# 342 dense tokens instead of 352, three lanes of 42 instead of four of 32, gate chunks of 18 instead of 16

## The chip, the core and the metric

The kernel runs on one core of a Trainium2 chip. The metric is the device time of one execution in microseconds (us). Of the kernel before there are three runs, with a median of 2845.26 us (2840.71 to 2845.80).

## What is computed

One decoder layer on 512 tokens of 2048 float32 channels: a convolution group and a sliding-window attention group, an output projection with a residual, and then the PEER channel mixer, which the change is about. PEER chooses 128 of 16384 single-neuron experts for each token (8 heads, 16 each) with a gate for each, and adds up their outputs:

```
def chunk_fn(args):                                    # xc: tokens, ec: chosen experts, gc: gates
    xc, ec, gc = args
    u_sel = jnp.take(peer_u, ec, axis=0)
    h = jnp.einsum("cd,chkd->chk", xc, u_sel)
    a = jax.nn.gelu(h, approximate=False) * gc
    v_sel = jnp.take(peer_v, ec, axis=0)
    return jnp.einsum("chk,chkd->cd", a, v_sel)
```

## The kernel before

The input projection, convolution, attention, output projection and the choice of experts run for all 512 tokens in the first third of the time. PEER then treats the tokens in two ways, at the same time.

**Dense tokens** (TD = 352). For these the kernel multiplies with all 16384 experts and lets a gate of zero remove those that were not chosen. TensorE (PE) works through 128 *expert tiles* (`expert_tile`, L957): a tile is 128 experts, two weight units of 1024 columns, 16 chunks of the channels, and three products a chunk (high by high, high by low, low by high parts), so 48 matmuls with TD columns each. The first 64 tiles (AHEAD = 8 groups of 8) only store their activations to DRAM (`H`). The other 64 tiles multiply them by the gates (`gated`, L998) and fold them straight into the output (`fold_group`, L1003: 8 steps a group, 48 matmuls a step, two banks that VectorE adds to `acc`, L1024). At the end the 8 stored groups come back and are folded. That is 12288 matmuls with TD columns, 6 lines (L965, L967, L968, L1014, L1016, L1017) with 2048 each.

**Weights.** `stream` (L129) loads pairs of units by SyncE's queue; for each unit ScalarE (ACT) writes the rounded high part `w_hi` (L153) and VectorE (DVE) the rest `w_lo` (L154), into rings of three buffers. A unit's `w_hi` can therefore only be written when TensorE is through with the unit three before it. 116 units are used ahead of expert tile 0, so tile e uses units 116+2e and 117+2e.

**Gates.** For the dense tokens `dense_gates` (L921) builds the dense gate rows, four tokens a call: VectorE makes one-hot rows `oh` (L930, two buffers), ScalarE scales four of them to `og` (L933), TensorE makes four products into one PSUM bank `gps` (L937), and ScalarE copies the bank into the chunk `gt` (L938). A chunk of GT = 16 tokens is written to DRAM (`G`, L940). 88 calls are handed out over the first 64 tiles by `pump`, which spends an allowance of 6.2 a tile on entries with a cost (3.4 a call); `drain` (L981) hands out the rest after tile 63. The pools of this stage are closed behind it; the pool `mg`, in which the first `hv` (the eviction of tile 64) lies, takes their place. Each group loads its gates `Gb` from `G` (L992). There are four `mm` banks, so tile 68 can start when tile 64 has been evicted.

**Gathered tokens.** The last 128 tokens have a token on each partition and take 128 gathers for `peer_u` and 128 for `peer_v`; NB = 32 further tokens are spread over LANES = 4 lanes of 32 partitions, with SB = 32 gathers for each table. A gather step (`gather_step`, L872) is one indirect load of 128 rows of 8 KB by GpSimd (POOL, L862) into one of three buffers (two `grow` and the unused one of `xrow`/`yrow`), and one pass of VectorE over 128x2048 (L884 for the products with `peer_u`, L894 for the sums with `peer_v`). There are STEPS = 320 steps. `step` (L951) spreads them over ticks 3 to 247 of 256; a tick is one expert tile or one fold step. What is left is handed out by L1061 after the last fold. Then the lanes are added up by four matmuls with `fold_s` (`yo`, L1072) and stored.

The order of the instructions on each engine is set at build time by a list scheduler that simulates the program; each engine then works through its own list strictly in order.

## Time and profile before

| | |
|---|---|
| median of three runs | 2845.26 us |
| the profiled execution | 2844.32 us |
| its span | 2842.5 us |
| TensorE busy | 2809.8 us (99%) |
| VectorE busy | 2367.0 us (83%) |
| ScalarE busy | 1209.9 us (43%) |
| GpSimd busy | 449.1 us (16%) |
| mean granted TensorE clock | 0.996 |
| moved by DMA | 761.06 MB |

Times in the rows are microseconds from the start of the span. A row of the timeline gives start, duration, engine, line and operation, output and inputs, how many instructions were merged, and in brackets the idle time of that engine before it with what ended it. In the tables by stretch each engine has its busy time and, as (x), the instructions that began there; then come the granted clock of TensorE (1.00 is full speed), the mean busy share of the 16 DMA engines, and what they moved.

### The profile page before, as it was taken

What the parts mean: (1) busy time and instruction counts of PE and PEld (TensorE: products, weight loads), DVE (VectorE), ACT (ScalarE), POOL (GpSimd) and SP (SyncE); (2) the same over time, 40 slices, a digit from 0 to 9 for tenths busy, and PEclk for the clock granted to TensorE, in tenths of its full rate; (3) what the DMA queues carried; (4) which work ended last, traced back from release to release, by engine and by line L of the source; (5) the groups of instructions that cost most, each with busy time, mean ns of one, the idle gap of its engine ahead of it and who ended that gap; (6) DMA issues with size and microseconds to landing.
All of it is one profiled execution on the core that took longest, in us unless ns stands there. A gap on an engine that the chain in (4) does not pass through costs nothing.

```text
span 2842.5 us, 42927 instructions
## 1 busy us (share of the span) xinstructions
PE 2809.8 (99%) x16995; PEld 2691.1 (95%) x16995; DVE 2367.0 (83%) x3586; ACT 1209.9 (43%) x1879; POOL 449.1 (16%) x337
## 2 busy tenths in 40 slices
PE   8999999999999999999999999999999999999999
PEld 8998877788899999999999999999999999999999
DVE  7888996569999988887777888788788888888886
ACT  5666434343343378786323333233333333333332
POOL 0000000000022212111222222222121221221231
PEclk9999999999999999999999999999999999999999
DMA  5222322433278889999899898888888898888886
GB/s 172 79 67 75 112 96 76 165 123 134 80 283 329 337 316 334 325 323 337 341 352 343 313 360 325 330 335 327 330 323 337 322 371 322 349 331 337 324 332 239
DMA packets 166762, 761.06 MB, mean 268 GB/s; under 512 B 14432, under 2 KB 66784, under 8 KB 90208
## 3 DMA queue, kind: packets, MB, share of 16 engines
q1 hardware_dynamic: 66432, 377.20, 35.5%
q0 software_dynamic: 46080, 335.56, 31.4%
q10 hardware_dynamic: 54048, 45.56, 4.9%
q8 instruction: 133, 2.18, 0.3%
q14 instruction: 69, 0.57, 0.1%
...
## 4 chain that ended last, share of the span: by engine, by line
PE 95%; DVE 3%; issue 1%; ACT 1%; DMA 0%; DVEq 0%; SPq 0%
PE mm L1014 11%; PE mm L1016 11%; PE mm L1017 11%; PE mm L967 11%; PE mm L968 11%; PE mm L965 11%; PE gps L937 3%; PE mm L600 2%; PE mm L601 2%; PE mm L817 2%; PE mm L819 2%; PE mm L818 2%; PE mm L512 2%; PE mm L511 2%; PE mm L510 2%; PE mm L599 2%
## 5 line engine op out<-in xcount | busy, mean ns | idle before, releaser
L153 ACT ACTIVATE w_hi<-w_raw 128x1024 fp32r<-128x1024 f32 x628 | 665.0, 1060 | 1289.9 <-PE mm L1016 630.5
L154 DVE TENSOR_TENSOR w_lo<-w_raw,w_hi 128x1024 fp32r<-128x1024 f32 x628 | 772.6, 1232 | 291.0 <-ACT w_hi L153 283.2
L967 PE MATMUL mm<-nl,w_hi 128*128 128x352 f32 x2048 | 664.5, 324 | 0.0
L965 PE MATMUL mm<-nh,w_hi 128*128 128x352 f32 x2048 | 662.9, 324 | 1.0 <-ACT w_hi L153 1.0
L968 PE MATMUL mm<-nh,w_lo 128*128 128x352 f32 x2048 | 660.2, 324 | 2.2 <-DVE w_lo L154 2.2
L1014 PE MATMUL mm<-ah,w_hi 128*128 128x352 f32 x2048 | 658.1, 323 | 2.7 <-DVE acc L1024 2.7
L1016 PE MATMUL mm<-al,w_hi 128*128 128x352 f32 x2048 | 660.2, 323 | 0.0
L1017 PE MATMUL mm<-ah,w_lo 128*128 128x352 f32 x2048 | 652.0, 322 | 1.4 <-DVE w_lo L154 1.4
L968 PEld LDWEIGHTS mm<-nh,w_lo 128*128 128x128 f32 x2048 | 384.8, 188 | 3.1 <-DVE w_lo L154 2.8
L1014 PEld LDWEIGHTS mm<-ah,w_hi 128*128 128x128 f32 x2048 | 384.1, 188 | 3.8 <-DVE acc L1024 2.7
L965 PEld LDWEIGHTS mm<-nh,w_hi 128*128 128x128 f32 x2048 | 385.3, 188 | 1.5 <-ACT w_hi L153 1.3
L967 PEld LDWEIGHTS mm<-nl,w_hi 128*128 128x128 f32 x2048 | 385.2, 188 | 0.1
L1017 PEld LDWEIGHTS mm<-ah,w_lo 128*128 128x128 f32 x2048 | 383.3, 188 | 2.0 <-DVE w_lo L154 2.0
L1016 PEld LDWEIGHTS mm<-al,w_hi 128*128 128x128 f32 x2048 | 384.7, 188 | 0.0
L862 POOL DMA_INDIRECT grow<-un,idx x87 | 119.5, 1373 | 855.1 <-DVE grow L884 403.5
L894 DVE SCALAR_TENSOR_TENSOR xrow<-grow,h,xrow 128x2048 f32<-128x2048 f32 x86 | 201.8, 2347 | 0.0
L884 DVE SCALAR_TENSOR_TENSOR grow<-grow,xrow 128x2048 f32<-128x2048 f32 x87 | 199.5, 2294 | 2.1 <-DMA grow<-un,idx 2.1
L862 POOL DMA_INDIRECT grow<-vn,idx x86 | 109.1, 1269 | 455.2 <-DVE xrow L894 439.3
L307 DVE SCALAR_TENSOR_TENSOR mix_c<-h,par,mix_c 128x512 f32<-128x512 f32 x240 | 173.7, 749 | 1.6
L1024 DVE TENSOR_TENSOR acc<-acc,mm 128x352 f32<-128x352 f32 x240 | 116.4, 518 | 65.8 <-PE mm L1017 65.7
L933 ACT ACTIVATE og<-oh,kt 128x128 f32<-128x128 f32 x352 | 110.4, 392 | 18.2 <-DVE oh L930 10.5
L930 DVE TENSOR_TENSOR oh<-iof,kt 128x1024 f32<-128x1024 f32 x88 | 105.9, 1221 | 11.7 <-PE gps L937 11.0
...
## 6 DMA issues: line engine op xcount, KB each, us to landing
w_raw<-ut SPq DMA_DIRECT2D x128, 1024.0 KB
w_raw<-vt SPq DMA_DIRECT2D x128, 1024.0 KB
...
```

The lines of the kernel that those rows point to most:

```text
L153: nc.scalar.activation(hi, raw, AF.Copy)
L154: nc.vector.tensor_tensor(lo, raw, hi.bitcast(FT), op=OP.subtract)
L307: nc.vector.scalar_tensor_tensor(mix_c[:, c], h[:, k:k + T], w, mix_c[:, c], op0=OP.mult, op1=OP.add)
L862: i = nc.gpsimd.indirect_dma_start(out=g, out_offset=None, in_=src, in_offset=bass.IndirectOffsetOnAxis(ap=at, axis=0))
L884: nc.vector.scalar_tensor_tensor(g, g, 1.0, rows["x"][:p], op0=OP.mult, op1=OP.mult, accum_out=h3[:p, k:k + 1])
L894: nc.vector.scalar_tensor_tensor(y, g, h3[:p, k:k + 1], y, op0=OP.mult, op1=OP.add)
L965: m = nc.tensor.matmul(bank, hi[:, s], nh[:, k, :TD], start=k == 0, stop=False)
L967: nc.tensor.matmul(bank, hi[:, s], nl[:, k, :TD], start=False, stop=False)
L968: nc.tensor.matmul(bank, lo[:, s], nh[:, k, :TD], start=False, stop=k == KC - 1)
L1014: m = nc.tensor.matmul(banks[j], hi[:, ws], ah[:, ee], start=ee == 0, stop=False)
L1016: nc.tensor.matmul(banks[j], hi[:, ws], al[:, ee], start=False, stop=False)
L1017: nc.tensor.matmul(banks[j], lo[:, ws], ah[:, ee], start=False, stop=ee == 7)
```

## The change

342 tokens are dense (TD), the other 42 (NB) go into three lanes of 42 partitions with 43 gathers each for either table (SB = 43; the 129th place is empty), so STEPS becomes 342. Every indirect load fetches 128 rows; the two partitions without a lane hold index 0 and a gate of zero. The gate chunk holds 18 tokens in 6 calls of three tokens (GQ), so there are 114 calls with a cost of 2.55. `h3` lies in another pool. Some slices start at partition 64, and buffers that lanes leave partly unwritten are cleared.

```diff
@@ -18,13 +18,13 @@
 T, D = 512, 2048
 KC = D // 128
 NT = T // 128
-TD = 352
+TD = 342
 TA = T - 128
 NB = TA - TD
-LANES = 128 // NB
-PB = LANES * NB
-SB = 128 // LANES
-GT = 16
+LANES = 3
+SB = 43
+GT = 18
+GQ = 3
 AHEAD = 8
 START = 2
 END = 247.0
@@ -666,7 +666,7 @@
         nc.scalar.activation(xrow[:, c4 * 512:c4 * 512 + 512], ps, AF.Copy)
         for src, to in ((pb, XB), (py, YB)):
             xb = xtp.tile([128, 512], FT, name="xb", bufs=1)
-            nc.scalar.activation(xb[128 - NB:], src[128 - NB:], AF.Copy)
+            nc.scalar.activation(xb[64:], src[64:], AF.Copy)
             nc.scalar.dma_start(to[:, c4 * 512:c4 * 512 + 512], xb[128 - NB:])
 
     X1 = [dram.tile([128, TD], FT, name=f"X{c}") for c in range(KC)]
@@ -791,15 +791,18 @@
         later(0.2, head_idx, h, low=True)
 
     def lane_lists():
-        ps_ = slice(128 - NB, 128)
+        ps_ = slice(64, 128)
+        nc.gpsimd.memset(idxb, 0)
+        nc.gpsimd.memset(GB3, 0.0)
         ib = kp.tile([128, 128], I32, name="ib")
         e1 = E1[ps_, 2].rearrange("p h k -> p (h k)")
         e2 = E2[ps_, 2].rearrange("p h k -> p (h k)")
-        ga = GA[ps_, 2].rearrange("p h k -> p (h k)")
+        ga = GA[128 - NB:, 2].rearrange("p h k -> p (h k)")
         nc.vector.scalar_tensor_tensor(ib[ps_], e1, 128.0, e2, op0=OP.mult, op1=OP.add)
         for l in range(LANES):
-            nc.scalar.dma_start(idxb[l * NB:l * NB + NB], ib[ps_, l * SB:l * SB + SB])
-            nc.scalar.dma_start(GB3[l * NB:l * NB + NB], ga[:, l * SB:l * SB + SB])
+            w = min(SB, 128 - l * SB)
+            nc.scalar.dma_start(idxb[l * NB:l * NB + NB, :w], ib[128 - NB:, l * SB:l * SB + w])
+            nc.scalar.dma_start(GB3[l * NB:l * NB + NB, :w], ga[:, l * SB:l * SB + w])
 
     for h in range(PH):
         kr = wqp.tile([128, 2, 128], FT, name="kr", bufs=2)
@@ -833,7 +836,7 @@
     G = dram.tile([16, 128, NCH, 8, GT], FT, name="G")
 
     pu = ctx.enter_context(tc.tile_pool(name="pu", bufs=1))
-    h3 = gat.tile([128, 128 + SB], FT, name="h3")
+    h3 = pu.tile([128, 128 + SB], FT, name="h3")
     rows = {"x": xrow, "y": None}
     STEPS = 2 * (128 + SB)
 
@@ -845,6 +848,7 @@
         if n == 128 + SB:
             nc.scalar.dma_start(t, YA)
         elif n == 128:
+            nc.gpsimd.memset(t, 0.0)
             for l in range(LANES):
                 nc.scalar.dma_start(t[l * NB:l * NB + NB], XB)
         else:
@@ -857,8 +861,7 @@
             g = pu.tile([128, D], FT, name="grow", bufs=2)
         else:
             g = gat.tile([128, D], FT, name=home[1], bufs=1)
-        at = idx[:, k:k + 1] if k < 128 else idxb[:PB, k - 128:k - 127]
-        g = g[:128 if k < 128 else PB]
+        at = idx[:, k:k + 1] if k < 128 else idxb[:, k - 128:k - 127]
         i = nc.gpsimd.indirect_dma_start(out=g, out_offset=None, in_=src,
                                          in_offset=bass.IndirectOffsetOnAxis(ap=at, axis=0))
         if after is not None:
@@ -878,20 +881,19 @@
                 nc.scalar.dma_start(out_r[NB:], rows["y"])
             rows["x" if n == 128 else "y"] = spare.pop(n)
             home.reverse()
-        p = 128 if k < 128 else PB
         if n < 128 + SB:
             g = gather(un, k, after)
-            nc.vector.scalar_tensor_tensor(g, g, 1.0, rows["x"][:p], op0=OP.mult, op1=OP.mult,
-                                           accum_out=h3[:p, k:k + 1])
-            if k % 16 == 15:
-                s = slice(k - 15, k + 1)
-                w = GA3[:, s] if k < 128 else GB3[:PB, k - 143:k - 127]
-                nc.scalar.activation(h3[:p, s], h3[:p, s], AF.Gelu)
-                nc.vector.tensor_tensor(h3[:p, s], h3[:p, s], w, op=OP.mult)
+            nc.vector.scalar_tensor_tensor(g, g, 1.0, rows["x"], op0=OP.mult, op1=OP.mult,
+                                           accum_out=h3[:, k:k + 1])
+            if k % 16 == 15 or k == 127 + SB:
+                s = slice(k - k % 16, k + 1)
+                w = GA3[:, s] if k < 128 else GB3[:, s.start - 128:s.stop - 128]
+                nc.scalar.activation(h3[:, s], h3[:, s], AF.Gelu)
+                nc.vector.tensor_tensor(h3[:, s], h3[:, s], w, op=OP.mult)
         else:
-            y = rows["y"][:p]
+            y = rows["y"]
             g = gather(vn, k, after)
-            nc.vector.scalar_tensor_tensor(y, g, h3[:p, k:k + 1], y, op0=OP.mult, op1=OP.add)
+            nc.vector.scalar_tensor_tensor(y, g, h3[:, k:k + 1], y, op0=OP.mult, op1=OP.add)
 
     done = [0]
 
@@ -921,30 +923,30 @@
 
     def dense_gates(q):
         pg, kt = gpl
-        c, part = divmod(q, GT // 4)
+        c, part = divmod(q, GT // GQ)
         if part == 0:
             gt[c] = pg.tile([128, 128, GT], FT, name="gt", bufs=2)
-        oh = pg.tile([128, 2, 4, 128], FT, name="oh", bufs=2)
-        og = pg.tile([128, 4, 128], FT, name="og", bufs=2)
-        ts = slice(4 * q, 4 * q + 4)
-        nc.vector.tensor_tensor(oh, iof[:, None, None, :].to_broadcast([128, 2, 4, 128]),
-                                kt[:, 0:2, ts, None].to_broadcast([128, 2, 4, 128]), op=OP.is_equal)
-        for i in range(4):
-            nc.scalar.activation(og[:, i], oh[:, 0, i], AF.Copy, scale=kt[:, 2, 4 * q + i:4 * q + i + 1])
+        oh = pg.tile([128, 2, GQ, 128], FT, name="oh", bufs=2)
+        og = pg.tile([128, GQ, 128], FT, name="og", bufs=2)
+        ts = slice(GQ * q, GQ * q + GQ)
+        nc.vector.tensor_tensor(oh, iof[:, None, None, :].to_broadcast([128, 2, GQ, 128]),
+                                kt[:, 0:2, ts, None].to_broadcast([128, 2, GQ, 128]), op=OP.is_equal)
+        for i in range(GQ):
+            nc.scalar.activation(og[:, i], oh[:, 0, i], AF.Copy, scale=kt[:, 2, GQ * q + i:GQ * q + i + 1])
         with tc.high_priority(offset=150):
-            ps = aux_bank([128, 4, 128], "gps")
-            for i in range(4):
+            ps = aux_bank([128, GQ, 128], "gps")
+            for i in range(GQ):
                 nc.tensor.matmul(ps[:, i], oh[:, 1, i], og[:, i], start=True, stop=True, skip_group_check=True)
-            nc.scalar.activation(gt[c][:, :, 4 * part:4 * part + 4].rearrange("p e t -> p t e"), ps, AF.Copy)
-        if part == GT // 4 - 1:
+            nc.scalar.activation(gt[c][:, :, GQ * part:GQ * part + GQ].rearrange("p e t -> p t e"), ps, AF.Copy)
+        if part == GT // GQ - 1:
             nc.scalar.dma_start(G[:, :, c].rearrange("g p e t -> p g (e t)"),
                                 gt.pop(c).rearrange("p (g e) t -> p g (e t)", e=8))
 
     later(0.0, open_gates, low=True)
     for t in range(3):
         later(0.4, transposes, t, low=True)
-    for q in range(TD // 4):
-        later(3.4, dense_gates, q, low=True)
+    for q in range(TD // GQ):
+        later(2.55, dense_gates, q, low=True)
 
     tick = [0]
 
@@ -1059,17 +1061,15 @@
             prepare(g + 1)
         fold_group(As.pop(g), 1.2, last=g == AHEAD - 1)
     gather_until(STEPS, None)
-    fold_s = mg.tile([128, LANES, NB], FT, name="fold_s")
-    nc.vector.tensor_copy(fold_s[:, 0], ident[:, 0:NB])
+    fold_s = mg.tile([128, NB], FT, name="fold_s")
+    nc.vector.tensor_copy(fold_s, ident[:, 0:NB])
     for l in range(1, LANES):
-        nc.vector.tensor_tensor(fold_s[:, 0], fold_s[:, 0], ident[:, l * NB:l * NB + NB], op=OP.add)
-    for l in range(1, LANES):
-        nc.vector.tensor_copy(fold_s[:, l], fold_s[:, 0])
+        nc.vector.tensor_tensor(fold_s, fold_s, ident[:, l * NB:l * NB + NB], op=OP.add)
     yo = pu.tile([128, D], FT, name="grow", bufs=2)
     for c4 in range(4):
         ps = aux_bank([128, 512], "yo")
         cs = slice(c4 * 512, c4 * 512 + 512)
-        nc.tensor.matmul(ps, fold_s.rearrange("p l n -> p (l n)"), rows["y"][:, cs], start=True, stop=True)
+        nc.tensor.matmul(ps[:NB], fold_s, rows["y"][:, cs], start=True, stop=True)
         nc.scalar.activation(yo[:NB, cs], ps[:NB], AF.Copy)
     nc.sync.dma_start(out_r[:NB], yo[:NB])
```

The new numbers also move instructions in the lists. In the lists below the lines of the changed kernel are L154 (`w_lo`), L153 (`w_hi`), L886 and L896 (the gather passes), L932 (`oh`), L935 (`og`), L939 (`gps`), L940 (`gt`), L942 (the write of `G`), L967/L969/L970 (an expert tile), L971 (eviction), L1002 (`gated`) and L1026 (`acc`).

TensorE, the last gate products. Before, in tile 61, between the products of the tile:

```order
L968 MATMUL mm<-nh,w_lo 128x352
L937 MATMUL gps<-og,oh 128x128
L965 MATMUL mm<-nh,w_hi 128x352
L937 MATMUL gps<-og,oh 128x128 x3
L967 MATMUL mm<-nl,w_hi 128x352
L968 MATMUL mm<-nh,w_lo 128x352
L965 MATMUL mm<-nh,w_hi 128x352
```

Now, from the end of tile 67 on; the row after the 48 is the first product of tile 68:

```order
L970 MATMUL mm<-nh,w_lo 128x342
L939 MATMUL gps<-og,oh 128x128 x3
L967 MATMUL mm<-nh,w_hi 128x342
L969 MATMUL mm<-nl,w_hi 128x342
L970 MATMUL mm<-nh,w_lo 128x342
L967 MATMUL mm<-nh,w_hi 128x342
L969 MATMUL mm<-nl,w_hi 128x342
L970 MATMUL mm<-nh,w_lo 128x342
L939 MATMUL gps<-og,oh 128x128 x48
L967 MATMUL mm<-nh,w_hi 128x342
```

The first gate products stand in tile 29 before and in tile 33 now, the last in tile 61 before and between tiles 67 and 68 now.

ScalarE at the same place. The last `w_hi` ahead of this piece is that of the first half of tile 69 (the 255th unit), and from it to the last write of `G` there are 45 `og` and 16 `gt`; this is the end of the piece, up to the next `w_hi`:

```order
L942 DMA G<-gt 128x16x144
L935 ACTIVATE og<-oh,kt 128x128
L940 ACTIVATE gt<-gps 128x3x128 x2
L935 ACTIVATE og<-oh,kt 128x128 x6
L940 ACTIVATE gt<-gps 128x3x128 x2
L935 ACTIVATE og<-oh,kt 128x128 x6
L940 ACTIVATE gt<-gps 128x3x128 x2
L942 DMA G<-gt 128x16x144
L971 ACTIVATE hv<-mm 128x342 x2
L188 ACTIVATE ah<-hv 128x342 x2
L971 ACTIVATE hv<-mm 128x342
L153 ACTIVATE w_hi<-w_raw 128x1024
```

The two evictions `hv` (tiles 64 and 65) wait for the last two writes of `G`, whose buffers lie where `hv` lies now. Before, the last write of `G` stands ahead of the eviction of tile 61.

VectorE, the end of the list. Before, one gather pass stands between the last `w_lo` and the last four `acc`, and none after:

```order
L894 SCALAR_TENSOR_TENSOR yrow<-grow,h_7303,yrow 128x2048
L1024 TENSOR_TENSOR acc<-acc,mm 128x352 x2
L154 TENSOR_TENSOR w_lo<-w_raw,w_hi 128x1024 x2
L894 SCALAR_TENSOR_TENSOR yrow<-grow,h_7303,yrow 128x2048
L1024 TENSOR_TENSOR acc<-acc,mm 128x352 x4
```

Now, from the last `w_lo` on; after the last two `acc`, which need the last product of the last fold step, 15 gather passes are left (the last four rows are the first six of them, and the other nine go on in the same pattern):

```order
L154 TENSOR_TENSOR w_lo<-w_raw,w_hi 128x1024 x2
L896 SCALAR_TENSOR_TENSOR yrow<-grow,h_7303,yrow 128x2048
L1026 TENSOR_TENSOR acc<-acc,mm 128x342 x2
L896 SCALAR_TENSOR_TENSOR yrow<-grow,h_7303,yrow 128x2048
L896 SCALAR_TENSOR_TENSOR yrow<-xrow,h_7303,yrow 128x2048
L1026 TENSOR_TENSOR acc<-acc,mm 128x342 x2
L896 SCALAR_TENSOR_TENSOR yrow<-grow,h_7303,yrow 128x2048 x2
L896 SCALAR_TENSOR_TENSOR yrow<-xrow,h_7303,yrow 128x2048
L896 SCALAR_TENSOR_TENSOR yrow<-grow,h_7303,yrow 128x2048 x2
L896 SCALAR_TENSOR_TENSOR yrow<-xrow,h_7303,yrow 128x2048
```

## Rows read from the trace of the kernel before

**Rows 1.** The page's part 1, busy time, share of the span, instructions.

```profile
PE 2809.8 (99%) x16995; PEld 2691.1 (95%) x16995; DVE 2367.0 (83%) x3586; ACT 1209.9 (43%) x1879; POOL 449.1 (16%) x337
```

**Rows 2.** Tables by stretch: later sweep, groups 8 to 15, stored groups, end.

```profile
905.00:1335.00 430.00, 428.55 (x2888) 427.90 (x2887) 364.00 (x389) 303.45 (x592) 91.22 (x59) 1.00 0.92 329
1335.00:2280.00 945.00, 942.28 (x5887) 941.17 (x5887) 756.22 (x739) 315.36 (x382) 197.50 (x160) 1.00 0.88 334
2280.00:2805.00 525.00, 523.57 (x3262) 522.99 (x3262) 454.25 (x480) 168.81 (x201) 123.72 (x79) 1.00 0.89 341
2805.00:2842.50 37.50, 33.28 (x195) 31.02 (x193) 19.81 (x18) 7.70 (x10) 0.94 (x1) 1.00 0.36 128
```

**Rows 3.** Groups by line: busy us, mean ns of one, then idle before.

```profile
L967 PE MATMUL mm<-nl,w_hi 128*128 128x352 f32 x2048 | 664.5, 324 | 0.0
L1017 PE MATMUL mm<-ah,w_lo 128*128 128x352 f32 x2048 | 652.0, 322 | 1.4 <-DVE w_lo L154 1.4
```

**Rows 4.** Timeline of PE: 22 matmuls in a row of 352 columns, first and last.

```profile
859.68 0.32 PE L965 MATMUL mm<-nh,w_hi 128*128 128x352 f32 x1
...
863.04 0.32 PE L965 MATMUL mm<-nh,w_hi 128*128 128x352 f32 x1
```

**Rows 5.** Timeline of PE: 17 matmuls in a row of 512 columns, first and last.

```profile
60.17 0.39 PE L510 MATMUL mm<-xh,w_hi 128*128 128x512 f32 x1
...
63.91 0.39 PE L511 MATMUL mm<-xl,w_hi 128*128 128x512 f32 x1
```

**Rows 6.** Chain that ended last: eight gate products, two instructions each.

```profile
1008.53 1.78 PE gps L937 x16
```

**Rows 7.** Timeline of ACT in the sweep: gate evictions, one-hot scalings, one `w_hi`.

```profile
1009.46 2.00 ACT L938 ACTIVATE gt<-gps 128x512 f32<-128x512 f32 x2 [1.25 <-PE gps L937]
...
1014.06 2.44 ACT L933 ACTIVATE og<-oh,kt 128x128 f32<-128x128 f32 x8
1016.59 1.06 ACT L153 ACTIVATE w_hi<-w_raw 128x1024 fp32r<-128x1024 f32 x1
```

**Rows 8.** Timeline of PE: its last gate products.

```profile
1332.24 0.83 PE L937 MATMUL gps<-og,oh 128*128 128x128 f32 x6
```

**Rows 9.** Timelines of ACT's and SP's queues: last `H` write, first `Gb`.

```profile
1354.91 0.34 ACTq L979 DMA_DIRECT2D H<-gl  x1
...
1361.10 0.33 SPq L992 DMA_DIRECT2D Gb<-G  x1
```

**Rows 10.** Tables by stretch, TensorE partly idle for five us, and after.

```profile
565.00:570.00 5.00, 3.72 (x22) 3.26 (x22) 1.66 (x4) 2.85 (x7) 0.00 (x0) 0.69 0.01 3
570.00:575.00 5.00, 5.00 (x18) 4.16 (x17) 3.93 (x6) 1.78 (x3) 0.00 (x0) 0.63 0.50 210
```

**Rows 11.** Timeline of DVE: two gather passes in a row; the last four `acc`.

```profile
2325.47 4.74 DVE L894 SCALAR_TENSOR_TENSOR xrow<-grow,h,xrow 128x2048 f32<-128x2048 f32 x2
...
2827.78 0.95 DVE L1024 TENSOR_TENSOR acc<-acc,mm 128x352 f32<-128x352 f32 x2
2834.41 1.00 DVE L1024 TENSOR_TENSOR acc<-acc,mm 128x352 f32<-128x352 f32 x2 [5.68 <-PE mm L1017]
```

**Rows 12.** Timeline of PE: the lane sums at the end.

```profile
2834.69 3.60 PE L1072 MATMUL yo<-yrow,fold_s 128*128 128x512 f32 x8
```

**Rows 13.** Timeline of POOL: the last gather.

```profile
2808.95 0.94 POOL L862 DMA_INDIRECT grow<-vn,idxb  x1 [6.73 <-DVE yrow L894]
```

**Rows 14.** Tables by half us: where its transfer ends.

```profile
2815.00:2815.50 0.50, 0.50 (x5) 0.50 (x4) 0.00 (x0) 0.00 (x0) 0.00 (x0) 1.00 0.44 158
2815.50:2816.00 0.50, 0.50 (x6) 0.50 (x5) 0.00 (x0) 0.38 (x1) 0.00 (x0) 1.00 0.01 3
```

**Rows 15.** Timelines of POOL and DVE: a gather that VectorE waited for.

```profile
1607.56 0.94 POOL L862 DMA_INDIRECT grow<-un,idx  x1 [10.62 <-DVE grow L884]
...
1618.68 2.29 DVE L884 SCALAR_TENSOR_TENSOR grow<-grow,xrow 128x2048 f32<-128x2048 f32 x1 [2.13 <-DMA grow<-un,idx]
```

**Rows 16.** The page's part 3, the queue of the gathers: packets, MB, share.

```profile
q0 software_dynamic: 46080, 335.56, 31.4%
```

## The prediction

> **What bounds the kernel now.** I first read the page's busy times, then the tables by stretch, then the groups and timelines of the places that the change touches. TensorE is busy 99% of the span [rows 1], at a granted clock of 1.00, the upper of its two levels (2.4 GHz), and through the whole PEER part it hardly stops: in the three stretches from 905 to 2805 us its idle time is 1900 - 1894.4 = 5.6 us [rows 2]. VectorE is at 83% there (1574 of 1900) and the DMA engines at 88 to 92% [rows 2], so both are covered by TensorE now, but not by much. The reader is to see two things: what is taken from the dense matmuls comes off the time one for one, and whatever makes TensorE stop, or work go on behind its last product, is added one for one.
>
> **Columns taken away.** The 12288 dense matmuls are six lines of 2048 [rows 3]; two of the six stand there. A row's 324 ns is the duration of a pipelined matmul; what counts is the distance between starts. 22 starts in a row take 863.04 - 859.68 = 3.36 us, 0.160 us each for 352 columns [rows 4]; 17 starts with 512 columns take 3.74 us, 0.234 us each [rows 5]. The two are in the ratio of their columns (0.455 and 0.457 ns a column), so I see no fixed part, and 10 columns fewer save 4.55 ns: 12288 x 4.55 ns = **-55.9 us**. The Trainium skill ("TensorE: Matmul & The Clock Gate", section "Back-to-back issue gap") gives N/2.4 + 2.5 ns for a warm matmul alone, 149 ns at 352 columns where the trace has 160. By it the saving would be 4.17 ns a matmul, 51.2 us instead of 55.9. The gates of ten tokens go too: a token's product is two instructions of 1.78/16 = 0.111 us [rows 6], 10 x 0.22 = **-2.2 us**.
>
> **The gate work between tiles 67 and 68.** Before, the last gate products ran at 1332 us, among the products of tile 61 [rows 8], three tiles ahead of the end of the stage. In the new list 48 of them (16 calls) stand together ahead of the first product of tile 68. ScalarE reaches this batch by the `w_hi` of the 255th unit, whose ring buffer is that of the second half of tile 67; so the batch starts when TensorE is through with tile 67. From there ScalarE has one `w_hi` of 1.06 us, 45 scalings at 2.44/8 = 0.305 (13.7 us) and 16 evictions [rows 7]. An eviction of 512 columns took 1.00 us; one of 384 lies between 0.75 (by columns) and 1.00; I take 0.8 as nearer to the columns, 12.8 us. That is 27.6 us. A call goes VectorE, ScalarE, TensorE, ScalarE through two buffers; the sweep shows up to 1.25 us of waiting in two calls [rows 7], so 0 to 10 us over the batch, and I take 4. Then the last write of `G` must land before `hv` takes its place. The nearest row is the last `H` write, 6.2 us from its issue until `Gb`, which takes its buffer, is issued [rows 9]; I bound it by 4 and 8 and take 6, since the write is larger (1.2 against 0.7 MB) but meets idle queues. With 0.6 us for the eviction, tile 68 starts 38.2 us after tile 67 ended. 48 x 0.222 = 10.7 us of that is gate products, which were paid before as well; 27.5 us is new idle time. Afterwards TensorE may meet a lower clock: after a stretch with 3.72 of 5 us busy the table shows 0.69 and 0.63 [rows 10], so part of the time at the lower level of 1.2 GHz; I put 3.5 us for it. VectorE's next `w_lo` stands behind `fold_s` and the first `gated` passes, which wait for `G` and for `Gb`; tile 68 and half of tile 69 (11.2 us) are already converted, which covers some 6 us of load and 6 us of passes closely, so 0 to 4 us more, taken as nothing. Sum **+31 us**, between 21 (no waits, short write, no clock loss) and 48 (all the upper ends).
>
> **The gathers behind the last product.** There are 342 gather steps instead of 320, and the list lets them fall behind: 15 passes stand behind the last `acc`, where before there was none. So they begin when TensorE has finished for good. `acc` ended 0.7 us after TensorE's last dense product (2834.41 + 1.00 against 2834.69) [rows 11, 12]. Two passes in a row take 4.74, so 2.37 us each [rows 11]. A buffer goes round in a pass, 0.3 us to GpSimd, and the load. For the load without the weights beside it I take the last gather: issued at 2808.95, transfer at an end by 2815.5, that is 6.5 us [rows 13, 14]. The round is 9.2 us for three gathers. The first three are loaded ahead; the fourth pass starts at 9.2, the seventh at 18.4, the tenth at 27.6, the thirteenth at 36.8, and the fifteenth ends at 43.9 us. The DMA engines allow that: a gather is 0.314 x 2842.5 / 320 = 2.79 us of all sixteen [rows 16]. Lower end: VectorE's own pace, 15 x 2.37 = 35.6 us. Upper end: the 11.1 us that a load took among the weights [rows 15], a round of 13.8 and 62 us in all. The lane sums took 3.60 us at the full clock [rows 12] and come now after 44 us of an idle TensorE, so I double them as at the lower level [rows 10], +3.6. Sum **+48 us**, between 36 and 66. The Trainium skill ("DMA: Bandwidth & Descriptors", section "Anatomy of one DMA — SWDGE (gpsimd) path") gives about 2.0 us plus the bytes at 436 GB/s for such a load, 4.4 us for its 1 MB, where the trace has 6.5. By that VectorE would set the pace and the sum would be about 8 us lower.
>
> **The rest.** 327 steps instead of 320 now lie beside a dense part that is 3% shorter, so the DMA share rises by about 0.05 and VectorE's from 0.83 to 0.86; TensorE idled 5.6 us under the present load [rows 2], and I put **+3 us**, from -5 (the present idle gone) to +20. The 26 more gate calls (each with three tokens instead of four), the clearing on GpSimd (16% busy [rows 1]), the narrower `acc` and `gated` passes and the smaller tables lie under TensorE and count nothing; if TensorE were not the bound, they would be a few us of either sign.
>
> **Sum.** -55.9 - 2.2 + 31 + 48 + 3 = +24 us, on a span of 2842.5, 2866.5; the execution's own time lies 1.8 us above its span, so 2868 us. That execution is 0.9 us below the median of the runs shown. About 0.2%, 5.7 us, is what a measurement of this kernel can tell from no change.
>
> **Rivals.**
> *The boundary costs almost nothing* (8%), the way to a faster kernel. If ScalarE and VectorE ran the batch beside tiles 65 to 67, only the write of `G` and the eviction would be left, 7 us, and with VectorE's pace in the tail (40 us with the lane sums) the sum is -58 + 7 + 40 = -11: 2833 us. It decides where boundary and tail together fall below 52 us. For it: ScalarE is busy only 303 of 430 us in the sweep [rows 2]. Against it: each engine keeps its order, and the `w_hi` ahead of the batch needs tile 67 to be finished.
> *The columns give nothing* (6%). If TensorE works in steps of 16 or 32 columns, 342 cost what 352 cost (both measured widths are multiples of 32 [rows 4, 5]), and the change doesn't do what it says: 2868 + 56 = 2924 us. The strict proportion speaks against it without excluding it; the rows of `ah`, now at multiples of 1368 bytes, could cost something of the same kind.
> *The loads become the bound* (9%). The steps come every 245 x 7.46 / 342 = 5.35 us. With 11.1 us of load the round of 13.8 allows 4.6; at 13.6 us it is 16.3, 5.43 a step, 0.08 too slow: VectorE waits, `w_lo` is late, and 327 x 0.08 = 26 us are added: 2894 us. For it: VectorE has already waited once with two buffers [rows 15]. Against it: TensorE hardly idles at a share of 0.92 [rows 2].
>
> **How the numbers follow.** The forecast has 77%. Its ends don't come together; 10 and 12 us down and 17, 18 and 17 us up, taken as independent, give about 2850 to 2898. With the third rival in, and the first two out, the range is 2846 to 2902. Faster: the first rival, 0.08. Within 0.2%: the lower ends of boundary and tail together, 0.08. Slower: 0.84.
>
> **What would show it.** Dense starts 0.1555 us apart (the columns); a gap on TensorE of some 27 us net ahead of tile 68, with ScalarE busy through it and the next `w_lo` after the first `gated`; 15 passes after the last `acc` over 36 to 62 us, with TensorE idle and the lane sums behind it at a lower clock. The prediction is wrong if tile 68 follows tile 67 within 15 us, if the tail is under 30 us, or if starts stay 0.160 us apart.

## The result, and the profile after

The changed kernel takes 2895.85 us (median of 4 runs, 2894.89 to 2898.28) against 2845.53 us for the kernel before on the same chip: ratio 1.0181, 95% interval 1.0169 to 1.0194. I had forecast 2868 us, so slower was right and +24 us was half of the +50 us measured. The profiled execution took 2896.28 us, its span is 2894.5 us, 52.0 us longer than before's, where the forecast had +24.

The page's part 1 of the changed kernel answers to [rows 1]:

```profile
PE 2777.1 (96%) x16975; PEld 2652.3 (92%) x16975; DVE 2409.3 (83%) x3642; ACT 1213.1 (42%) x1896; POOL 498.7 (17%) x362
```

The tables by stretch answer to [rows 2] (window; length; busy us and count on PE, PEld, DVE, ACT, POOL; granted clock; DMA share; GB/s):

```profile
905.00:1335.00 430.00, 425.40 (x2865) 425.04 (x2865) 367.35 (x426) 277.90 (x525) 98.98 (x65) 1.00 0.97 339
1335.00:2280.00 945.00, 920.47 (x5838) 916.81 (x5837) 757.03 (x750) 344.04 (x464) 202.46 (x158) 0.99 0.88 330
2280.00:2805.00 525.00, 517.63 (x3286) 515.96 (x3286) 451.27 (x481) 169.45 (x203) 121.30 (x79) 1.00 0.91 341
2805.00:2894.50 89.50, 31.57 (x172) 26.63 (x170) 56.19 (x33) 6.84 (x9) 26.98 (x18) 0.68 0.76 245
```

TensorE was idle 5.6 us in the first three stretches before; now it is idle 4.6 + 24.5 + 7.4 = 36.5 us there, and 57.9 us in the last. The waits of PE name where (released by; us in total, times, longest):

```profile
PE yo L1072 <- DVE yrow L896: 52.7, 1, 52.7
PE gps L939 <- ACT og L935: 15.9, 11, 4.6
PE mm L967 <- ACT hv L971: 9.5, 1, 9.5
PE mm L1019 <- DVE w_lo L154: 7.4, 6, 4.8
```

**Columns.** The timeline of PE, 28 products of 342 columns in a row, first and last, answers to [rows 4]:

```profile
1507.72 0.32 PE L969 MATMUL mm<-nl,w_hi 128*128 128x342 f32 x1
...
1511.95 0.32 PE L969 MATMUL mm<-nl,w_hi 128*128 128x342 f32 x1
```

That is 4.23 us over 27 distances, 156.7 ns each, where 352 columns took 160.0; other quiet stretches of the sweep and of the fold have 156.6 to 156.7 as well. A product saves 3.3 ns and not 4.55: 12288 x 3.33 = 40.9 us instead of 55.9.

**Boundary.** Tables by stretch, then the timelines of ACT (with its queue) and of PE where tile 68 begins:

```profile
1335.00:1375.00 40.00, 33.18 (x206) 31.85 (x204) 31.48 (x33) 29.93 (x63) 8.51 (x6) 0.93 0.96 310
1375.00:1400.00 25.00, 11.07 (x58) 9.85 (x58) 9.95 (x13) 16.08 (x39) 1.41 (x1) 0.77 0.67 196
1400.00:1405.00 5.00, 5.00 (x24) 5.00 (x23) 0.60 (x2) 0.05 (x1) 0.00 (x0) 0.67 0.63 260
```

```profile
1390.74 0.37 ACTq L942 DMA_DIRECT2D G<-gt  x1
1398.70 0.80 ACT L971 ACTIVATE hv<-mm 128x342 f32<-128x342 f32 x2 [7.99 <-DMA G<-gt]
```

```profile
1362.62 0.83 PE L939 MATMUL gps<-og,oh 128*128 128x128 f32 x6
...
1387.80 1.95 PE L939 MATMUL gps<-og,oh 128*128 128x128 f32 x12 [1.15 <-ACT og L935]
1399.21 0.66 PE L967 MATMUL mm<-nh,w_hi 128*128 128x342 f32 x1 [9.46 <-ACT hv L971]
```

The batch begins at 1362.62, right behind tile 67, and tile 68 at 1399.21, 36.6 us later. TensorE follows ScalarE through the gate calls; then ScalarE waits 8.0 us for the last `G` write and TensorE for the eviction behind it. In the three windows it idles 6.8 + 13.9 = 20.8 us (2.2 of them three tiles earlier, before a single gate call), and by the granted clock it loses about 33.2 x 0.07 + 11.07 x 0.23 + 5 x 0.33 = 6.5 us of its busy time: some 27 us.

**Tail.** The last dense product ends at 2830.6 us, 4.1 us earlier than before; from there to the end of the span it takes 63.9 us where it took 7.8, so 56.1 more. Timelines of DVE (the first passes, one in the middle and the last of 15), POOL (the gathers of two of these passes) and PE:

```profile
2831.32 2.35 DVE L896 SCALAR_TENSOR_TENSOR yrow<-grow,h,yrow 128x2048 f32<-128x2048 f32 x1 [0.18 <-issue]
2836.26 2.35 DVE L896 SCALAR_TENSOR_TENSOR yrow<-grow,h,yrow 128x2048 f32<-128x2048 f32 x1 [2.59 <-DMA grow<-vn,idxb]
2840.88 2.35 DVE L896 SCALAR_TENSOR_TENSOR yrow<-xrow,h,yrow 128x2048 f32<-128x2048 f32 x1 [2.26 <-DMA xrow<-vn,idxb]
...
2864.59 2.35 DVE L896 SCALAR_TENSOR_TENSOR yrow<-grow,h,yrow 128x2048 f32<-128x2048 f32 x1 [1.73 <-DMA grow<-vn,idxb]
...
2880.89 2.35 DVE L896 SCALAR_TENSOR_TENSOR yrow<-xrow,h,yrow 128x2048 f32<-128x2048 f32 x1 [0.86 <-DMA xrow<-vn,idxb]
```

```profile
2830.43 0.94 POOL L865 DMA_INDIRECT xrow<-vn,idxb  x1 [0.30 <-issue]
...
2856.86 0.94 POOL L865 DMA_INDIRECT grow<-vn,idxb  x1 [3.29 <-DVE yrow L896]
```

```profile
2883.30 5.98 PE L1072 MATMUL yo<-yrow,fold_s 128*42 128x512 f32 x8 [52.70 <-DVE yrow L896]
```

Fifteen passes take 51.9 us, 3.46 each. Only the first finds its rows loaded: the second and the third wait 2.59 and 2.26 us. The load into `xrow` issued at 2830.43 was ready for the pass at 2840.88, 10.4 us later, although no weights ran beside it any more. That is the longest; the last twelve took 5.7 to 9.7 us from issue to pass, 7.4 on average (one of them 2856.86 to 2864.59). The lane sums took 5.98 us and not 3.60 [rows 12].

**The ledger of the 52.0 us:** the dense part began 4.2 us earlier (why is open), columns -40.9, tail +56.1. That leaves +41 for what stopped or slowed TensorE within the dense part. Read there are 37 us: 27 at the boundary and 10 of added idle time elsewhere. The other 4 us are not accounted for, and the gates of ten tokens can't be told apart in it.

### The profile page after: what moved, and what is told of

It reads as the page before. It is cut to its first block, busy times and chain, and to the rows that moved or that the text cites. A ratio compares the mean times of both kernels' runs of the same rounds, so it can differ in the third digit from the quotient of the medians.

```text
span 2894.5 us, 43016 instructions
## 1 busy us (share of the span) xinstructions
PE 2777.1 (96%) x16975; PEld 2652.3 (92%) x16975; DVE 2409.3 (83%) x3642; ACT 1213.1 (42%) x1896; POOL 498.7 (17%) x362
## 4 chain that ended last, share of the span: by engine, by line
PE 87%; DVE 5%; DMA 4%; issue 2%; ACT 1%; POOL 1%; ACTq 0%; POOLq 0%; DVEq 0%
PE mm L967 10%; PE mm L970 10%; PE mm L969 10%; PE mm L1019 10%; PE mm L1016 10%; PE mm L1018 10%; PE gps L939 2%; PE mm L600 2%; PE mm L601 2%; PE mm L820 2%; PE mm L512 2%; PE mm L511 2%; PE mm L822 2%; PE mm L510 2%; PE mm L821 2%
## 5 line engine op out<-in xcount | busy, mean ns | idle before, releaser
L153 ACT ACTIVATE w_hi<-w_raw 128x1024 fp32r<-128x1024 f32 x628 | 665.6, 1061 | 1252.5 <-PE mm L1018 625.6
L154 DVE TENSOR_TENSOR w_lo<-w_raw,w_hi 128x1024 fp32r<-128x1024 f32 x628 | 771.4, 1231 | 254.2 <-ACT w_hi L153 244.1
L967 PE MATMUL mm<-nh,w_hi 128*128 128x342 f32 x2048 | 656.7, 321 | 11.4 <-ACT hv L971 9.5
L969 PE MATMUL mm<-nl,w_hi 128*128 128x342 f32 x2048 | 656.0, 320 | 0.0
L1016 PE MATMUL mm<-ah,w_hi 128*128 128x342 f32 x2048 | 651.5, 319 | 3.8 <-DVE acc L1026 3.8
L970 PE MATMUL mm<-nh,w_lo 128*128 128x342 f32 x2048 | 653.7, 321 | 1.2 <-DVE w_lo L154 1.1
L1018 PE MATMUL mm<-al,w_hi 128*128 128x342 f32 x2048 | 653.2, 319 | 0.0
L1019 PE MATMUL mm<-ah,w_lo 128*128 128x342 f32 x2048 | 641.6, 320 | 7.4 <-DVE w_lo L154 7.4
L967 PEld LDWEIGHTS mm<-nh,w_hi 128*128 128x128 f32 x2048 | 386.2, 189 | 12.4 <-ACT hv L971 9.6
L970 PEld LDWEIGHTS mm<-nh,w_lo 128*128 128x128 f32 x2048 | 385.5, 189 | 2.3 <-DVE w_lo L154 2.1
L969 PEld LDWEIGHTS mm<-nl,w_hi 128*128 128x128 f32 x2048 | 386.2, 189 | 0.1
L865 POOL DMA_INDIRECT grow<-un,idx x87 | 136.0, 1563 | 805.5 <-DVE grow L886 464.9
L896 DVE SCALAR_TENSOR_TENSOR xrow<-grow,h,xrow 128x2048 f32<-128x2048 f32 x87 | 204.2, 2347 | 0.0
L886 DVE SCALAR_TENSOR_TENSOR grow<-grow,xrow 128x2048 f32<-128x2048 f32 x87 | 200.0, 2299 | 1.0 <-DMA grow<-un,idx 1.0
L1026 DVE TENSOR_TENSOR acc<-acc,mm 128x342 f32<-128x342 f32 x240 | 114.8, 508 | 69.7 <-PE mm L1019 69.6
L932 DVE TENSOR_TENSOR oh<-iof,kt 128x768 f32<-128x768 f32 x114 | 107.0, 956 | 24.8 <-PE gps L939 24.3
L940 ACT ACTIVATE gt<-gps 128x384 f32<-128x384 f32 x114 | 98.3, 898 | 57.5 <-PE gps L939 41.1
```

Source lines behind the costliest of these rows:

```text
L153: nc.scalar.activation(hi, raw, AF.Copy)
L154: nc.vector.tensor_tensor(lo, raw, hi.bitcast(FT), op=OP.subtract)
L865: i = nc.gpsimd.indirect_dma_start(out=g, out_offset=None, in_=src, in_offset=bass.IndirectOffsetOnAxis(ap=at, axis=0))
L886: nc.vector.scalar_tensor_tensor(g, g, 1.0, rows["x"], op0=OP.mult, op1=OP.mult, accum_out=h3[:, k:k + 1])
L896: nc.vector.scalar_tensor_tensor(y, g, h3[:, k:k + 1], y, op0=OP.mult, op1=OP.add)
L967: m = nc.tensor.matmul(bank, hi[:, s], nh[:, k, :TD], start=k == 0, stop=False)
```

## The experiments

`e10`, `e11` and `e13` were run four times, the others once; beside each stands the kernel before on the same chip, 2842 to 2844 us. Of a kernel run once, only differences of 5 us and more are read. `e1` to `e14` are the names below; `e1`, `e2`, `e6` and `e14` leave work out.

**What a column costs.** `e1`, the kernel before with mixed widths:

```
+        w = WS[e % 8]
...
-                m = nc.tensor.matmul(bank, hi[:, s], nh[:, k, :TD], start=k == 0, stop=False)
+                c = w if first else TD
+                m = nc.tensor.matmul(bank[:, :c], hi[:, s], nh[:, k, :c], start=k == 0, stop=False)
...
-                nc.tensor.matmul(bank, hi[:, s], nl[:, k, :TD], start=False, stop=False)
+                nc.tensor.matmul(bank[:, :w], hi[:, s], nl[:, k, :w], start=False, stop=False)
```

> The kernel before, in which all but the first product into each PSUM bank (one of 48 in a tile, two of 48 in a fold step) take fewer columns: 352, 348, 346, 344, 342, 340, 338, 336 in the eight tiles of a group, 352, 334, 332, 330, 328, 326, 324, 320 in the eight fold steps. The columns left out are computed in the first product only. Read is the distance between starts in quiet stretches. Theory A (TensorE streams in steps of 8 columns, so that 342 cost what 344 cost): 160.0 ns at 352, 348 and 346; 156.4 at 344, 342, 340 and 338; 152.7 at 336, 334, 332 and 330; 149.1 at 328, 326 and 324; 145.5 at 320. Theory B (strictly by columns, as I forecast, and something else in the changed kernel took 1.2 ns a product): 158.2 at 348, 155.5 at 342, 152.7 at 336, 145.5 at 320, with 0.9 ns less at every step of two. Theory C (a fixed part, 0.333 ns a column): 158.7 at 348, 156.7 at 342, 154.7 at 336, 149.3 at 320. The whole time is no criterion here, since the order of the other engines' work shifts with the shorter products; by the products alone it would be 67 us shorter by A and 81 by B.

Measured, mean distance of starts between 1400 and 2270 us, some 300 per width: 160.2 ns at 352, 159.7 at 348, 156.7 at 346, 156.0 at 344, 154.7 at 342, 154.4 at 340, 156.5 at 338, 153.4 at 336, 153.0 at 334, 152.3 at 332, 152.5 at 330, 150.1 at 328, 149.3 at 326, 149.6 at 324, 146.2 at 320. No theory holds at every width. Steps of 8 (A) come nearest, 0.8 ns off on the average against 1.2 for the line of proportion (B), but 346, 342 and 340 lie 1.7 to 3.3 ns under their step and 338 lies above 340. The line is too low at most widths, by 2.9 ns at 338. C is out: the slope from 320 to 352 is 0.44 ns a column and not 0.333. At 342 tiles stood at 153.7 to 153.9 or at 156.7 to 157.0. The whole took 2809.7 us.

`e6` took one width for each group (`w = WG[e // 8 % 3]`, the same in the fold):

> The kernel before, with all but the first product into each bank cut to 342, 344 or 340 columns, one width for a whole group of eight tiles or eight fold steps, the next width for the next group (the columns left out are in the first product only). In the run with mixed widths a product of 342 columns stood at two levels, 153.7 to 153.9 ns in five tiles and 156.7 to 157.0 in two, 344 took 155.7 to 155.9 (once 157.8) and 340 took 154.3. Theory A (the width itself costs it, in a stream of its own kind): 342 takes 156.7 ns here as in the changed kernel, more than 344 with 155.8 and 340 with 154.4. Theory B (strict proportion, and the changed kernel's own buffers or loads added 1.2 ns a product): 342 takes 155.5 or less here, between 340 and 344.

Measured 2802.8 us, 40.0 under before: as the mean width is 342, this is the gain of the columns without gathers, gates or tail, and it agrees with the -40.9 read above. Two neighbouring tiles of the sweep, timeline of PE, the first and the last product of 342 columns of each:

```profile
1465.62 0.32 PE L970 MATMUL mm<-nl,w_hi 128*128 128x342 f32 x1
...
1472.67 0.32 PE L971 MATMUL mm<-nh,w_lo 128*128 128x342 f32 x1
1472.83 0.32 PE L968 MATMUL mm<-nh,w_hi 128*128 128x352 f32 x1
1472.98 0.32 PE L970 MATMUL mm<-nl,w_hi 128*128 128x342 f32 x1
...
1480.19 0.32 PE L971 MATMUL mm<-nh,w_lo 128*128 128x342 f32 x1
```

Each holds 46 distances: 7.05 us are 153.3 ns, 7.21 us are 156.7 ns, and the tiles of this group alternate. In the fold behind 2290 us whole groups averaged 157.5 and 158.0 ns at 342 columns, 156.4 to 157.8 at 344 and 155.0 to 156.9 at 340. So A holds as far as 342 can cost more than 344; it is not one price.

`e14` put one narrower product into each tile of the changed kernel (`w = WL[e // 8 % 3] if k == KC - 1 else TD`):

> The changed kernel in which the last of the 48 products of a sweep tile is 340 columns wide in the groups 1, 4, 7, 10, 13 and 334 wide in the groups 2, 5, 8, 11, 14, and 342 as ever in the others (the missing columns of that one product are left out). Products of 342 columns stood at 153.3 to 153.9 ns or at 156.7 ns, and alternated from tile to tile where one product a tile had 352 columns; in the changed kernel they stood at 156.7 nearly always. Theory A (one product of another width turns the stream from one level to the other): tiles alternate in the groups with an odd product, mean 155.2 ns, and stay at one level in the others. Theory B (the levels come from elsewhere, as from the weights' or the banks' place): 156.7 in all groups. By A some 128 x 2/3 x 47/2 x 3.3 ns = 6.6 us less in the whole, by B 0.

Measured 2904.1 us, and 156.7 ns in all groups, with or without the odd product: theory B. What sets the level stays open; that the changed kernel runs at the upper one is shown. The new row length of `ah`, which the prediction names as a possible cost, is not needed for it: the sweep reads `nh`, whose rows the change leaves as they were, and has 156.7 too.

**The tail alone.** `e2` leaves out the last 15 steps (`while done[0] < min(n, STEPS - 15)`):

> The changed kernel without its last 15 of 342 gather steps (the sums of 15 of the last 43 weight rows of the laned tokens are left out). Everything ahead of TensorE's last dense product stays in the same order. Theory A (the 15 passes behind the last acc stand on the path one for one): 52 us of passes go, and the lane sums run at the full clock again (-3), so 2896 - 55 = 2841 us, between 2836 and 2846. Theory B (the end is set by loads that have been late since long before, so that others would be waited for in their place): less than 30 us go, 2866 or more.

Measured 2837.8 us, 58 under the changed kernel: theory A, the passes are paid one for one. Without them columns, gates, boundary and the rest come to within 5 us of the kernel before.

**The boundary.** `e3` hands the gathers out from tick 12 (`START = 12`):

> The changed kernel with its first gather handed out at tick 12 instead of 2. In the list the last gate product then stands among the products of tile 63, as no batch ahead of tile 68, and 26 passes instead of 15 stand behind the last acc. Theory A (boundary and tail are two terms that trade with each other): the boundary gives back 28 us, 11 more passes at 52/15 = 3.47 us cost 38, so 2896 + 10 = 2906 us, between 2898 and 2914, and TensorE passes from tile 67 to tile 68 with under 5 us of idle time. Theory B (the change of stage itself stops TensorE, with its loads of Gb, Hb and the last G write, and not the bunched gate calls): the gap of some 20 us at tile 68 stays, 2934 us.

Measured 2913.8 us, at A's upper end. Tables by stretch:

```profile
1335.00:1400.00 65.00, 65.00 (x424) 65.00 (x424) 50.00 (x56) 25.57 (x35) 11.81 (x10) 1.00 0.94 361
1400.00:1440.00 40.00, 26.68 (x150) 25.92 (x149) 28.68 (x31) 7.41 (x7) 12.60 (x8) 0.89 0.88 336
```

The gap at tile 68 is gone, so the batch had made it. But 13.3 us of idle time now stand in the first fold steps, all of it waits for `acc` (15.9 us against 3.8). Taking off the 36.2 us by which the wait for the tail grew (88.9 against 52.7), 18 us came back, not the 28 of theory A.

`e12` removes the batch without moving a gather:

```
-        oh = pg.tile([128, 2, GQ, 128], FT, name="oh", bufs=2)
-        og = pg.tile([128, GQ, 128], FT, name="og", bufs=2)
+        oh = pg.tile([128, 2, GQ, 128], FT, name="oh", bufs=3)
+        og = pg.tile([128, GQ, 128], FT, name="og", bufs=3)
```

> The changed kernel with three buffers instead of two for oh and og (the one-hot rows of the gate calls and their scaled copies). In the list the last gate product then stands at tile 60 instead of in a batch ahead of tile 68, with the first gather at tick 2 as before; 16 passes instead of 15 stand behind the last acc. Theory A (the batch alone is what stops TensorE between tiles 67 and 68, and its price is the idle time and the low clock there, 28 us): 2896 - 28 + 3.5 for one more pass, 2868 to 2876, and under 5 us of idle time at tile 68. Theory B (the boundary gives back only part, as with the first gather at tick 12, where the gap went and 13 us of new waits for acc came some 40 us later; net 17): 2879 to 2888, with those waits in the first fold steps.

Measured 2892.0 us: 4 us came back, 7 without the one more pass (the wait for the tail grew from 52.7 to 55.7), less than either theory said, though this is one run. TensorE ran without a stop from 1375 to 1425 us, but it idled 16.6 us between 905 and 1335 (4.6 in the changed kernel), at a granted clock of 0.98. The table of that stretch, and the wait of ACT that grew there:

```profile
905.00:1335.00 430.00, 413.39 (x2792) 411.83 (x2792) 363.76 (x429) 293.27 (x606) 91.95 (x60) 0.98 0.95 325
```

```profile
ACT gt L940 <- DMA G<-gt: 33.2, 6, 12.1
```

In the changed kernel that line is 8.6 us, once. With gate calls closer together, ScalarE stands before a `gt` buffer whose write hasn't landed, and TensorE's next gate product stands behind it. So the batch came late by the list's order, but earlier gate calls meet writes that have not landed. That the DMA engines (share 0.97 there in the changed kernel, 0.95 here) could not take them faster is likely and not shown.

**Can the 15 passes be carried beside the products?** Eight kernels hold all the work and take the tail away, or all but 2 to 4 passes of it. `e4` ties the order on VectorE:

```
...
+            if passes and passes[0][0] + LAG <= tick[0]:
+                tc.add_manual_dep(low.ins, passes.popleft()[1],
+                                  mybir.DependencyInfo(mybir.DependencyClass.NoSync, mybir.DependencyReason.DATA),
...
```

> The changed kernel, all work in it, with one more rule for the list: a w_lo that is handed out at a tick must stand behind every gather pass that was handed out six or more ticks earlier (an order on VectorE alone, no wait is added). No pass stands behind the last acc then; the gate batch ahead of tile 68 stays. Theory A (the tail comes from the order in the list; buffers and DMA engines can carry 1.40 steps a tick beside the weights): 2896 - 55, plus up to 12 us for w_lo that now wait for a late gather: 2841 to 2853, likeliest 2846. Theory B (the load is the bound: three buffers and the DMA engines don't carry 1.40 steps a tick, the tail only showed it): the time comes back as waits of w_lo for the gathers, 2875 us or more.

Measured 2865.4 us, between the two. The tail is gone, and these are three of the waits between 2280 and 2805 us:

```profile
PE mm L1028 <- DVE w_lo L158: 26.8, 15, 10.5
DVE acc L1035 <- PE mm L1028: 32.3, 22, 4.7
DVE yrow L906 <- DMA xrow<-vn,idxb: 9.5, 2, 9.0
```

One pass waited 9.0 us for a gather into the old output row; GpSimd had to wait 3.8 us with it until the row was written out. All other waits of passes for loads come to 8 us there, so most of the rest was not the loads. So the next two kept the rule and spaced it evenly:

```
-            while len(passes) > 1 and passes[1][0] + LAG <= tick[0]:
+            while passes and passes[0][0] + LAG <= (i - N_SMALL) / 2:
...
-        passes.append((tick[0], p.ins.name))
+        passes.append((START + n * (END - START) / STEPS, p.ins.name))
```

> The changed kernel, all work in it, with the first gather at tick 12 (no gate batch at tile 68) and an order rule by fractions of a tick: each gather pass has a due time, the 342 of them evenly spaced from tick 12 to tick 248, and the first w_lo due six ticks later or more must stand behind it on VectorE. Before this, with whole ticks and lag 6 from tick 2, the tail went but w_lo waited 26.8 us in the fold, 9 us of it at the switch of the output row and the rest where two or three passes stood in a row. Theory A (order is all that cost the time; evenly spaced passes meet loads that have landed): 2896 - 55 (tail) - 29 (boundary) and 5 to 20 us of waits for late gathers: 2817 to 2832, likeliest 2824. Theory B (three buffers don't carry a step in 5.15 us beside the weights, whatever the order): waits of 27 us or more as before, 2840 or more.

> As the run with even spacing from tick 12, but from tick 10 to tick 252 and a lag of three ticks: a step in 5.28 us instead of 5.15, last gate products at tile 65.6 instead of 62.6, and passes due up to tick 255. Theory A (order and spacing): the slower pace gives fewer waits in the fold, 3 to 15 us, and the last G write comes within 3 tiles of tile 68, so up to 4 us there: 2815 to 2832. Theory B (the buffers' round is the bound): waits of 27 us or more, 2840 or more.

Measured 2870.6 and 2868.1 us: both times theory B's number. Two more gave the fold five gather buffers instead of three, with the first gather at tick 12 (`e8`) and at tick 2 (`e9`):

```
...
+        if late:
+            m = done[0] % 5
+            g = pu.tile([128, D], FT, name="grow", bufs=2) if m < 2 else late[0].tile([128, D], FT, name="grow2", bufs=3)
...
```

> The changed kernel, all work in it, first gather at tick 12, and three more gather buffers in the memory that comes free when the sweeps are over (the last 64 of 256 ticks): there the gathers go round through five buffers instead of three, and the old output row is no longer gathered into. No order rule. In the list no pass is left behind the last acc, and the last gate products stand at tile 63. Theory A (what holds the gathers up in the last 64 ticks is the number of buffers, not the DMA engines): against the run with tick 12 alone, 2914, the tail of 26 passes goes with the slow lane sums (89 + 4 us), up to 15 us come back as loads that collide in the fold: 2821 to 2836, likeliest 2828. Theory B (the DMA engines are the bound there; with the order rules the time came back as waits of w_lo): 2850 to 2870, with more than 25 us of w_lo waits behind 2280 us.

> The same three late buffers, but the first gather at tick 2 as in the changed kernel: the gate batch at tile 68 stays as it is. Theory A: 2896 - 55 + up to 12 = 2841 to 2853, and 10 to 20 us more than the run with late buffers and tick 12 (there the boundary gave back some 17 us net, since new waits for acc came behind it). Theory B (order rules and buffers make no difference, the loads are the bound): 2860 to 2880. Theory C (gathers from tick 12 on have to be caught up later, which costs in the fold what the boundary gave): both runs within 5 us of each other.

Measured 2876.0 and 2901.9 us, both beyond every theory; the two are 26 us apart, so C is out. The table by stretch of `e9` between 2280 and 2805 us, both waits of DVE that the view lists there, and its timeline:

```profile
2280.00:2805.00 525.00, 477.57 (x2922) 470.72 (x2922) 463.11 (x467) 152.85 (x188) 155.19 (x98) 0.96 0.92 359
```

```profile
DVE acc L1030 <- PE mm L1023: 45.7, 29, 4.3
DVE w_lo L154 <- ACT w_hi L153: 15.6, 14, 2.8
```

```profile
2604.58 0.98 DVE L1030 TENSOR_TENSOR acc<-acc,mm 128x342 f32<-128x342 f32 x2 [1.15 <-PE mm L1023]
2605.48 2.35 DVE L154 TENSOR_TENSOR w_lo<-w_raw,w_hi 128x1024 fp32r<-128x1024 f32 x2
2607.75 4.74 DVE L900 SCALAR_TENSOR_TENSOR yrow<-grow,h,yrow 128x2048 f32<-128x2048 f32 x2
2613.50 0.98 DVE L1030 TENSOR_TENSOR acc<-acc,mm 128x342 f32<-128x342 f32 x2 [1.02 <-PE mm L1023]
2614.40 2.35 DVE L154 TENSOR_TENSOR w_lo<-w_raw,w_hi 128x1024 fp32r<-128x1024 f32 x2
```

No gather is waited for any more, and yet TensorE idles 47.4 us in these 525. The step takes 2613.50 - 2604.58 = 8.92 us instead of 7.52: two passes push the `w_lo` pair behind `acc`, `acc` waits for the step that TensorE is in, and TensorE then waits for the `w_lo` behind it. My theory A (buffers) falls, and so does B as I had put it: by this timeline, and not by a run that changes it alone, it is the order on VectorE. The next two therefore squeezed passes in only between 1420 and 2280 us (`MID = (80, 94, 188, 262)` with `END = 225.0`, then `(80, 107, 188, 262)` with `END = 235.0`):

```
...
+            due = (i - N_SMALL) / 2
+            if MID[0] <= due <= MID[2]:
+                tc.add_manual_dep(low.ins, passes[int(MID[1] + (MID[3] - MID[1]) * (due - MID[0]) / (MID[2] - MID[0])) - 1],
...
```

> The changed kernel, all work in it, first gather at tick 12, three gather buffers as always, and the order rule only from tick 80 to tick 188 (about 1420 to 2280 us): there each w_lo stands behind as many gather passes as lie on a line from 94 at tick 80 to 262 at tick 188 (1.56 a tick against 1.31 in the list without a rule). In the fold behind it the list keeps its own pace of some 1.15 a tick, and 2 passes are left behind the last acc. Theory A (VectorE and the queue order leave room for more passes in the sweeps between 1500 and 2280 us alone, where TensorE never stopped in the changed kernel at a VectorE share of 0.82; in the fold, at 0.86 to 0.90, each more pass delays a w_lo): 2914 - 93 (tail of the run with tick 12) + 7 (two passes) + 3 to 12 us of waits in the middle: 2831 to 2840, so under the kernel before by 5 to 14 us. Theory B (a pass more costs the same wherever it stands; DMA engines or the buffers' round): 2855 or more, with 20 us or more of w_lo waits between 1420 and 2280 us.

> The same with the first gather at tick 2: the rule goes from 107 passes at tick 80 to 262 at tick 188 (1.44 a tick), 2 passes behind the last acc, and the gate batch ahead of tile 68 is there (54 products instead of 48). Theory A: the result without the last 15 steps, 2838, + 7 for two passes, + 2 for the larger batch, + 0 to 6 us of waits in the middle: 2847 to 2853; some 15 us above the run with tick 12. Theory B: 2865 or more.

Measured 2887.8 us (ratio 1.0158, 1.0141 to 1.0175) and 2863.1 us (1.0070, 1.0048 to 1.0092). The stretch from 1500 to 2280 us, `e11`, then `e10`:

```profile
1500.00:2280.00 780.00, 779.53 (x4973) 779.26 (x4973) 652.45 (x620) 263.25 (x319) 223.34 (x142) 1.00 0.89 344
```

```profile
1500.00:2280.00 780.00, 752.74 (x4744) 748.27 (x4743) 656.04 (x624) 250.18 (x304) 245.12 (x152) 0.99 0.91 349
```

142 gathers in 780 us cost 0.5 us of TensorE's time, 152 cost 27.3: `e10` asked for more than the stretch holds, and its time is theory B's. In `e11` A's mechanism is right for the middle, and its time is missed by 10 us elsewhere: 29.4 us of idle time at the larger boundary (24.5), 8.0 in the tail. `e13` adds the three one-hot buffers to a rule of this kind (`MID = (76, 100, 188, 260)`, `END = 241.0`):

> The same three buffers for oh and og, and the order rule from tick 76 to tick 188 at 1.43 passes a tick (the pace at which TensorE idled 0.5 us between 1500 and 2280 us in the run with the rule from tick 2), 4 passes left behind the last acc. Theory A (1.43 a tick fit between 1420 and 2280 us; the fold and the stretch ahead of tile 68 keep the list's own pace): 2872 - 12 x 3.47 = 2830, between 2824 and 2842, under the kernel before. Theory B (squeezed passes give back half at best, as in the runs with lag and mid rules: 52 us of tail bought 25 to 33): 2848 to 2856.

Measured 2860.8 us (1.0062, 1.0045 to 1.0079), theory B or worse: TensorE idled 4.5 us in the middle, but 11.3 between 905 and 1335 us as in `e12`, 12.3 between 1335 and 1500, and 14.8 for the passes left at the end. No version that does all the work beats the kernel before.

All runs built on the changed kernel together, instructions of GpSimd begun in a stretch (all but one or two are gathers) against TensorE's idle time there:

| stretch | gathers: idle us |
|---|---|
| 1500 to 2280 | before 133: 0; changed, e3, e14 135: 0; e2, e9, e12 136: 0; e4, e8 138: 0; e11 142: 0.5; e13 142: 4.5; e7 143: 7.6; e5 144: 3.7; e10 152: 27.3 |
| 2280 to 2805 | before 79: 1.4; e12, e14 79: 5.8; changed, e2 79: 7.4; e13 80: 6.4; e3 80: 7.7; e11 80: 8.5; e10 81: 11.2; e4 92: 26.9; e7 92: 31.4; e5 95: 32.3; e8 95: 38.2; e9 98: 47.4 |

In the fold each gather beyond 79 costs 1.5 (`e4`) to (47.4 - 7.4) / 19 = 2.1 us of idle time (`e9`). Idle time is not the whole price: in the changed kernel TensorE began 3286 products there and in `e9` 2922, 364 fewer, which at 156.7 ns is some 57 us; the granted clock there was 0.96 instead of 1.00. Counted so, a gather more in the fold costs 2.0 (`e4`, `e5`) to 3.0 us (`e9`), against 3.46 in the tail. The middle took some seven more for nothing in the best case (`e11`; `e13`, with as many, idled 4.5 us). So a better order mends part of the tail: 30 to 35 of the 50 us came back (`e4`, `e11`, `e13`). No order tried brought all of it back.

## Why the prediction was right or wrong

**What bounds the kernel:** right. TensorE is busy in 96% of the span; the columns (`e6`) and the tail (`e2`) came off the time one for one. The stop at the boundary did not when it was taken away, since others came in its place.

**"I see no fixed part, and 10 columns fewer save 4.55 ns":** this term failed, -55.9 against -40.9 (alone, in `e6`: -40.0). The line through 352 and 512 columns was drawn from two widths that both lie on it; 342 costs 1.2 ns more, and 12288 of them are 15 us, over half of the miss of 28 (52.0 against +24). The Trainium skill ("TensorE: Matmul & The Clock Gate", section "Back-to-back issue gap") would have 4.17 ns a product; the trace has 3.33, so that rule came nearer and missed as well. My rival of steps of 16 or 32 columns is out: 340 columns took 154.4 ns in `e1` and 352 took 160.2.

**The gate work between tiles 67 and 68:** right in place and mechanism, and near in size: +31 forecast, some 27 found, 36.6 us from tile 67 to tile 68 where I had 38.2. TensorE followed ScalarE through the batch, which was done after 28.1 us (I had 31.6), the last `G` write took 8.0 us (I had 6), and the clock came back at 0.67. That the two errors nearly cancel is luck. What I had not asked is what the same work would do elsewhere: without the batch only 7 to 18 us return.

**"For the load without the weights beside it I take the last gather: ... 6.5 us":** the second term that failed, +48 against +56. Two steps of it were wrong. "The first three are loaded ahead": only the first was, and the fourth pass began 12.5 us after the last `acc` and not 9.2, since the buffers had only just come free. And up to three gathers were under way at a time, where the row that I took has one (beside some 0.7 MB of output): the last twelve loads averaged 7.4 us, so the twelve passes from the fourth on took 39.6 us and not 34.7. The estimate by the Trainium skill ("DMA: Bandwidth & Descriptors", section "Anatomy of one DMA — SWDGE (gpsimd) path"), 2.0 us plus the bytes at 436 GB/s, 4.4 us, is farther off: it would be one load alone, and no run here shows that. Lane sums: +3.6 forecast, 2.4 found.

**The rest:** +3, from -5 to +20, was the third, small miss, some +10 that can be read: the stops between 905 and 1335 us (4.6 against 1.5) and in the fold (7.4 against 1.4), and what stood around the boundary.

**The rivals.** That the boundary costs nothing fell. That the loads become the bound had 9%, with VectorE waiting 0.08 us a step; in the changed kernel this does not happen, since the list never asks for that pace. But when the pace was asked for (`e4` to `e11`), it could not be had in the fold or at the gates, by the waits read there for VectorE's order and the `G` writes more than for the loads.
